# Two more seven-product pairs in the down projection, six raw weight buffers and rings of five split weights

## The chip, the cores and the metric

The kernel runs on one core of one Trainium2 chip. The metric is device time in microseconds (us) of one execution. Times below come from three timed runs and from one profiled execution of the kernel before.

## The reference

The reference is one decoder layer in float32 on 256 tokens and 16 meta tokens. What matters here is its last part, the SwiGLU feed-forward network on 256 tokens with width 2048 and 5632 hidden channels:

```python
u = rmsnorm(h, attn_norm_w[l])
proj = u @ w_in[l]
...
h = h + jnp.concatenate([o_a, o_d], axis=-1) @ w_out[l]
u = rmsnorm(h, ffn_norm_w[l])
h = h + (jax.nn.silu(u @ w_gate[l]) * (u @ w_up[l])) @ w_down[l]
```

All weights are float32 and each is read once from memory.

## The kernel before

**A product in three matmuls.** Every float32 operand is split into `hi` (rounded to the matmul's type) and `lo` (the rest). A product of two blocks is then three matmuls: hi by hi, hi by lo, lo by hi. The activations are split once. A weight tile of 128 x 1024 numbers (512 KB) goes through three steps: a DMA that SP issues brings it into a buffer `raw` (`load_to`, L261), ACT casts it to `hi` (L274), and DVE subtracts to get `lo` (L275). There are `WR` = 4 buffers `raw` in one ring. The pairs of `hi` and `lo` stand in rings of `WS` = 4, and from the SwiGLU on `WS2` = 2 more, so six. `next_w` hands the next split weight to the matmuls; on each call it splits ahead as far as the ring goes and issues loads ahead (`load_to(pos[3] + WR - 1)`).

**Seven products for eight.** In the SwiGLU (chunks of 512 hidden channels, `chunk`) and in the down projection (two passes p = 0 and p = 1 over two column tiles of 512 each), the weights come in pairs: two channel blocks by two column tiles. `block` (L1367) multiplies such a pair with the two token blocks. An ordinary pair takes two split weights (called w, w in what follows), each used in 4 products, so 8 products or 24 matmuls. The pairs named in `SEVEN` (SwiGLU) and `DSEVEN` (down: 7, 9, 11, 13, 15, 17, 19 of the 22 pairs in each pass) take 7 products or 21 matmuls by a Strassen-like scheme. For that DVE forms sums of the two raw tiles (L291 to L294: `t` twice, then `s` twice, 128 x 512 each), and four split weights are made, in this order: the first raw tile (g), half of the second (u), `t`, `s`. It also needs sums of the activations. They are made by `side_forms` (L1318 to L1330: seven DVE instructions and two ACT casts) ahead of the pass, and used by both passes.

**What sets the order.** A generator-based task list (`tasks`) places side work between products while the program is written. Instructions on ACT and SP stay in that order; those on PE and DVE are put in their final order by a scheduler. Each engine then runs its own list in order, so an instruction that waits holds up all behind it on its engine. SP's list of DMAs is in order too.

**The matmuls** of chunks and of down stand on L1381, those of the first chunk on L1199. The first chunk is computed as two plain streams (gate, up), and its end, `ffn_task` (L1306 multiplies, `to_hT` transposes on L1277), runs while PE has begun the second chunk. Between the two passes of down, `down_mid` and `down_end` (L1504, L1516) finish the first two column tiles, SP writes them out (L1518), and `fetch_x1` loads the residual for the next two (L1484).

Of the kernel before, what the change touches and what calls it, by code (L numbers as in the profile page):

```python
# [8 lines left out]
F32 = mybir.dt.float32  # L9
# [6 lines left out]
P = 128  # L16
# [5 lines left out]
FFN = 5632  # L22
# [3 lines left out]
NCH = FFN // 512  # L26
# [3 lines left out]
KC = (0, 72, 144, T)  # L30
R1, R2 = 12, 10
WR, WS = 4, 4
WS2 = 2
WHOLE = 8
SEVEN = (2, 4, 6)
DSEVEN = (7, 9, 11, 13, 15, 17, 19)
# [130 lines left out]
def layer(tc, xT, aw, x, w_in, w_ba, w_out, w_gate, w_up, w_down, cmask, dist, par, out):  # L167
# [3 lines left out]
    def pool(name, bufs=1, space=None):  # L171
        cm = tc.tile_pool(name=name, bufs=bufs, **({"space": space} if space else {}))
        return cm, cm.__enter__()
# [8 lines left out]
    cm_w, wp = pool("wp")  # L182
# [7 lines left out]
    tasks = Tasks(PER_STEP)  # L190
# [13 lines left out]
    def act(out_, in_, func, **kw):  # L204

        act_table("silu_and_others" if func == AF.Silu else "natural_log_exp_and_others")
        S.activation(out_, in_, func, **kw)

    def mark(k, n=1):
        done[k] = done.get(k, 0) + n  # L210

    def at_least(k, n):
        return lambda: done.get(k, 0) >= n
# [20 lines left out]
    def w_tile(wv, q, c):  # L234
        return wv[:, 2 * q:2 * q + 2, 512 * c:512 * (c + 1)], 2, 512
# [4 lines left out]
    forms = [("w", i) for i in range(len(order))]  # L240
    for c in range(1, NCH):
        for q in range(KT // 2):
            i = len(order)
            order += [w_tile(wv, q, c) for wv in (wg_v, wu_v)]
            forms += [("w", i), ("w", i + 1)] if q not in SEVEN else [("g", i), ("u", i), ("t", i), ("s", i)]
    for c in (0, 2):
        for q in range(FFN // P // 2):
            i = len(order)
            order += [w_tile(wd_v, q, c + j) for j in range(2)]
            forms += [("w", i), ("w", i + 1)] if q not in DSEVEN else [("g", i), ("u", i), ("t", i), ("s", i)]  # L250
    raws, ready, sums_ = {}, {}, {}

    pos = [0, 0, 0, 0]
    more = []

    def load_to(n, parts=1, eng=nc.sync):
        while pos[0] < min(n, len(order)):
            src, a, b = order[pos[0]]
            raw = wp.tile([P, a, b], F32, tag="raw", bufs=WR, name=f"raw{pos[0]}")
            for i in range(0, a, a // parts):  # L260
                eng.dma_start(out=raw[:, i:i + a // parts], in_=src[:, i:i + a // parts])  # L261
            raws[pos[0]] = raw
            pos[0] += 1

    def split(raw, n, a, b, parts=1, rows=slice(0, None)):

        k = n % (WS + WS2) if more else 0
        if k < WS:
            hi, lo = (wp.tile([P, a, b], F32R, tag=t, bufs=WS, name=f"{t}{n}") for t in ("hi", "lo"))
        else:  # L270
            hi, lo = (more[0].tile([P, a, b], F32R, tag=f"{t}2", bufs=WS2, name=f"{t}{n}") for t in ("hi", "lo"))
        for j in range(0, a, a // parts):
# [31 lines left out]
    def next_w():  # L304
        i = pos[2]
        pos[2] += 1
        split_to(i + WS + (WS2 if more else 0))
        load_to(pos[3] + WR - 1)
        return ready.pop(i)


# [3 lines left out]
    nc.sync.dma_start(out=xr[0][:, 0:1, :], in_=xT[:, 0:1, :])  # L315
    nc.sync.dma_start(out=aw_sb, in_=aw)
    load_to(1, 2, S)

    act_table("natural_log_exp_and_others")
# [61 lines left out]
    for k in range(KT):  # L381
        src, w = xr[k // 8][:, k % 8, :], aw_sb[:, k:k + 1]
# [870 lines left out]
    hT = {}  # L1253
# [45 lines left out]
    def ffn_task(c, b, pg, pu):  # L1299
        g_ = yield from fpool[1].get(512)  # L1300
        act(g_, pg, AF.Silu, scale=rr[:, b:b + 1])
        mm.free()
        yield at_least(f"up{c}", 1)
        yield 1
        ps = pu[b]
        V.scalar_tensor_tensor(g_, ps, rr[:, b:b + 1], g_, ALU.mult, ALU.mult)  # L1306
        mm.free()
        yield 2
        yield from to_hT(c, b, g_)


# [2 lines left out]
    def side_forms(key, h, l, sh, sl):  # L1314

        v = yield from fpool[1].get(2, SEQ)
        w = yield from fpool[1].get(4, P)
        V.tensor_tensor(v, h, l, ALU.add)  # L1318
        a11, a21, a12, a22 = v[:, 0, 0:P], v[:, 0, P:SEQ], v[:, 1, 0:P], v[:, 1, P:SEQ]
        V.tensor_tensor(w[:, 0], a21, a22, ALU.add)  # L1320
        V.tensor_tensor(w[:, 1], w[:, 0], a11, ALU.subtract)
        V.tensor_tensor(w[:, 2], a11, a21, ALU.subtract)
        V.tensor_tensor(w[:, 3], a12, w[:, 1], ALU.subtract)
        yield 2
        h1, l1 = h[:, 0, P:SEQ], l[:, 0, P:SEQ]
        S.copy(h1, w[:, 0])
        S.copy(sh, w[:, 1:4])
        yield 1
        V.tensor_tensor(l1, w[:, 0], h1, ALU.subtract)
        V.tensor_tensor(sl, w[:, 1:4], sh, ALU.subtract)  # L1330
        fpool[1].free(2)
        sides[key] = [(h1, l1)] + [(sh[:, i], sl[:, i]) for i in range(3)]
        mark(f"side{key}")

    def side_tiles(i):
        return [fpool[0].tile([P, 3, P], F32R, tag=f"{n}{i}", name=f"{n}{i}") for n in ("sh", "sl")]
# [27 lines left out]
        yield 10  # L1364
        yield from to_hT(c, b, h_)

    def block(c, name, nq, seven, lhs, need, mid, end):  # L1367

        ring, other = rings[c % 2], rings[(c + 1) % 2]
        tasks.until(lambda: ring.live == 0)  # L1370
        x = [ring.now() for _ in range(4)]
        y = []
        n = nq - len(seven)
        left = {("x", i): 3 * (2 * n + (len(seven) if i < 3 else 0)) for i in range(4)}
        left.update({("y", i): 3 * len(seven) for i in range(4)})
        todo = dict(left)

        def product(bank, a, w):
            for l, r in ((a[0], w[0]), (a[0], w[1]), (a[1], w[0])):
                first, todo[bank] = todo[bank] == left[bank], todo[bank] - 1  # L1380
                PE.matmul((x if bank[0] == "x" else y)[bank[1]], l, r, start=first, stop=todo[bank] == 0)  # L1381

        for q in range(nq):
            k = 2 * q
            if need:
                tasks.until(need(k))
            if q not in seven:
                for col in range(2):
                    hi, lo = next_w()
                    for i in range(2):  # L1390
                        for b in range(2):
                            product(("x", 2 * col + b), lhs(k + i, b), (hi[:, i], lo[:, i]))
                            tasks.step()
                    if q == nq - 1:
                        end(col, x)
                continue
            if not y:
                tasks.until(lambda: other.live == 0)
                y += [other.now() for _ in range(4)]
            tasks.until(at_least(f"side{(name, q)}", 1))  # L1400
            s1, s2_, s3, s4 = sides[name, q]
            plan = (((("y", 0), lhs(k, 0), 0), (("x", 0), lhs(k + 1, 0), 1)), ((("x", 2), s4, 1),),
                    ((("y", 3), s1, 0), (("y", 2), s3, 1)), ((("y", 1), s2_, 0), (("x", 1), lhs(k + 1, 1), 1)))
            for part in plan:
                hi, lo = next_w()
                for bank, a, i in part:
                    product(bank, a, (hi[:, i], lo[:, i]))
                    tasks.step()
            if q == seven[-1]:
                mid(y)  # L1410
# [32 lines left out]
    for b in range(2):  # L1443
        tasks.spawn(ffn_task(0, b, pg[b], pu), urgent=True)
    pu += stream(range(KT - 4), lhs_u, last=False)
    for i, q in enumerate(SEVEN):
        k = slice(2 * q, 2 * q + 2)
# [61 lines left out]
    def down_end(p, b, c, ps):  # L1509
# [8 lines left out]
            nc.sync.dma_start(out=out[P * b:P * (b + 1), o:o + w], in_=r_)  # L1518
        rings[(NCH + p) % 2].free()

    def down_side(i, q):
        if i < len(SEVEN):
            sh, sl = side_tiles(i)
        else:
            if i == len(SEVEN):

                yield at_least(f"hT{NCH - 1}", 3)
                t = fpool[0].tile([P, 6 * P], F32R, tag=f"hT{NCH - 1}", name=f"side{q}")
            else:
                o = 8 * SEQ + 6 * P * (i - len(SEVEN) - 1)  # L1530
                t = rest[:, o:o + 6 * P]
            sh, sl = (t[:, 3 * P * j:3 * P * (j + 1)].rearrange("p (a b) -> p a b", b=P) for j in range(2))
        k = slice(2 * q % 4, 2 * q % 4 + 2)
        c = q // 2
        yield at_least(f"hT{c}", 2 if c < WHOLE else 3)
        h, l = (hT[c][:, 0], hT[c][:, 1]) if c < WHOLE else hT[c]
        yield from side_forms(("h", q), h[:, k, :], l[:, k, :], sh, sl)
# [3 lines left out]
    for i, q in enumerate(DSEVEN):  # L1541
        tasks.spawn(down_side(i, q), delay=24)
    tasks.spawn(fetch_x1(0), delay=24)
    for p in range(2):
        def end(col, x):
            for b in range(2):
                tasks.spawn(down_end(p, b, col, x[2 * col + b]), urgent=True)

        def mid(y):
            tasks.until(lambda: fpool[1].live <= 1)  # L1550
            t = [fpool[1].now((512,)) for _ in range(3)]
            S.copy(t[0], y[0])
            tasks.spawn(down_mid(p, y, *t), delay=0, urgent=True)

        block(NCH + p, "h", FFN // P // 2, DSEVEN, lhs_h, need_h, mid, end)
        if p == 0:
            tasks.spawn(fetch_x1(1), delay=12)
    tasks.until(lambda: not tasks.list)
# [66 lines left out]
```

## Time and profile before

| | value |
|---|---|
| median of three runs | 1223.23 us (1222.27 to 1226.79) |
| profiled execution | 1224.38 us, its span 1222.6 us |
| mean granted TensorE clock | 1.000 |
| PE busy | 1209.2 us (99%), 7316 matmuls |
| DVE busy | 983.6 us (80%) |
| ACT busy | 692.3 us (57%) |
| DMA | 228.54 MB, mean 187 GB/s |

The span is the time from the first to the last instruction. Busy time of PE is modelled from the starts of pipelined matmuls. In time order the span holds the mixer with its projections (to about 510 us), the first chunk (to 558 us), ten more chunks (to 983 us), pass p = 0 of down (to 1099 us) and pass p = 1 (to 1218 us). "Released by" in a wait means the instruction or DMA whose end let the waiting one start.

### The profile page before, as it was taken

The numbers are of one execution on the slowest core, as the hardware profiler recorded it, in microseconds if no ns is written. First come the engines' busy times: TensorE is split into PE (matmuls) and PEld (weight loads), VectorE is DVE, ScalarE is ACT, GpSimd is POOL, SyncE is SP. The second block draws the span as 40 slices with busy tenths as digits, with TensorE's granted clock in tenths as the row PEclk, the third lists the DMA queues.
The fourth block names the chain that finished last, engine by engine and source line by source line (L and its number), as shares of the span: only waits on it lengthen the run. The fifth ranks groups of instructions, "written<-read, shape, count | busy, mean of one in ns | idle before, by whom it ended". The sixth has DMA issues, their size and how long they took to land.

```text
span 1222.6 us, 19223 instructions
## 1 busy us (share of the span) xinstructions
PE 1209.2 (99%) x7316; PEld 1060.0 (87%) x7316; DVE 983.6 (80%) x1573; ACT 692.3 (57%) x1087; POOL 6.1 (0%) x14
## 2 busy tenths in 40 slices
PE   9999999999999999999999999999999999999998
PEld 7999999999999988887888888888888888888876
DVE  7989974686676666668889988998998899886686
ACT  7674465275776665455555556555555665553552
POOL 0000000000000000000000000000000000000000
PEclk9999999999999999999999999999999999999999
DMA  8466564344544645685665665566566565567543
GB/s 293 124 207 195 145 187 121 112 124 145 172 140 139 229 162 178 191 277 167 196 206 186 195 218 190 192 204 217 166 208 216 187 211 197 201 225 276 181 164 133
DMA packets 151869, 228.54 MB, mean 187 GB/s; under 512 B 11736, under 2 KB 72672, under 8 KB 151264
## 3 DMA queue, kind: packets, MB, share of 16 engines
q1 hardware_dynamic: 151232, 226.78, 57.4%
q8 instruction: 57, 0.93, 0.3%
q10 hardware_dynamic: 544, 0.52, 0.1%
q14 instruction: 36, 0.29, 0.1%
HBM read 221.83 MB, written 5.45 MB: 186 GB/s over the span
## 4 chain that ended last, share of the span: by engine, by line
PE 85%; DVE 7%; DMA 4%; ACT 2%; issue 1%; SPq 0%; DVEq 0%; ACTq 0%
PE aux L1381 25%; PE mm L1152 23%; PE mm L1381 21%; PE mm L1199 10%; DVE lo L275 3%; DMA raw<-in_w_down_dram 3%; ACT hi L274 1%; PE aux L1100 1%; PE aux L1055 1%; DMA raw<-in_w_in_dram 0%; PE mm L1277 0%; DVE s L293 0%; DMA raw<-in_w_up_dram 0%; DVE r L581 0%; PE aux L1277 0%
## 5 line engine op out<-in xcount | busy, mean ns | idle before, releaser
L274 ACT CAST hi<-raw 128x1024 fp32r<-128x1024 f32 (+1 forms) x412 | 405.1, 996 | 325.0 <-PE mm L1152 93.3
L275 DVE TENSOR_TENSOR lo<-raw,hi 128x1024 fp32r<-128x1024 f32 (+1 forms) x412 | 470.6, 1153 | 141.6 <-ACT hi L274 139.1
L1152 PE MATMUL mm<-xh,hi 128*128 128x272 f32 (+2 forms) x896 | 258.4, 289 | 0.0
L1152 PE MATMUL mm<-xl,hi 128*128 128x272 f32 (+2 forms) x896 | 255.9, 286 | 0.9 <-DVE xl L384 0.6
L1152 PE MATMUL mm<-xh,lo 128*128 128x272 f32 (+2 forms) x896 | 255.0, 286 | 1.0 <-DVE lo L275 1.0
L1152 PEld LDWEIGHTS mm<-xl,hi 128*128 128x128 f32 x896 | 168.5, 188 | 2.2 <-DVE xl L384 2.0
L1152 PEld LDWEIGHTS mm<-xh,hi 128*128 128x128 f32 x896 | 168.6, 188 | 2.1 <-issue 1.5
L1152 PEld LDWEIGHTS mm<-xh,lo 128*128 128x128 f32 x896 | 168.2, 188 | 1.6 <-DVE lo L275 1.4
L1381 PE MATMUL aux<-hi,uh 128*128 128x512 f32 x260 | 101.6, 391 | 0.0
L1381 PE MATMUL mm<-hi,uh 128*128 128x512 f32 x260 | 101.6, 391 | 0.0
L1381 PE MATMUL aux<-hi,ul 128*128 128x512 f32 x260 | 101.3, 390 | 0.0
L1381 PE MATMUL mm<-hi,ul 128*128 128x512 f32 x260 | 101.2, 389 | 0.0
L1381 PE MATMUL aux<-lo,uh 128*128 128x512 f32 x260 | 101.2, 389 | 0.0
L1381 PE MATMUL mm<-lo,uh 128*128 128x512 f32 x260 | 101.2, 389 | 0.0
L1381 PE MATMUL aux<-hi,hT 128*128 128x512 f32 x216 | 70.2, 389 | 0.0
L1381 PE MATMUL mm<-hi,hT 128*128 128x512 f32 x216 | 70.0, 389 | 0.0
L274 ACT CAST hi<-s 128x1024 fp32r<-128x1024 f32 x44 | 46.3, 1053 | 38.0 <-DVE s L294 34.5
L291 DVE TENSOR_TENSOR t<-raw,raw 128x512 f32<-128x512 f32 x44 | 30.2, 687 | 38.7 <-DMA raw<-in_w_down_dram 25.2
L274 ACT CAST hi<-t 128x1024 fp32r<-128x1024 f32 x44 | 46.3, 1053 | 26.2 <-DVE t L292 11.3
L1381 PEld LDWEIGHTS aux<-hi,ul 128*128 128x128 f32 x260 | 48.8, 188 | 10.2
L1381 PEld LDWEIGHTS mm<-hi,ul 128*128 128x128 f32 x260 | 48.8, 188 | 10.2
L1381 PEld LDWEIGHTS mm<-hi,uh 128*128 128x128 f32 x260 | 48.8, 188 | 10.0
(418 smaller groups left out, 2046.8 us busy)
## 6 DMA issues: line engine op xcount, KB each, us to landing
raw<-in_w_in_dram SPq DMA_DIRECT2D x111, 512.0 KB, 3.6
raw<-in_w_gate_dram SPq DMA_DIRECT2D x88, 512.0 KB, 3.7
raw<-in_w_up_dram SPq DMA_DIRECT2D x88, 512.0 KB, 4.4
raw<-in_w_down_dram SPq DMA_DIRECT2D x88, 512.0 KB, 4.6
raw<-in_w_out_dram SPq DMA_DIRECT2D x32, 512.0 KB, 4.2
x<-x1d SPq DMA_DIRECT2D x8, 256.0 KB, 4.8
xr<-in_xT_dram SPq DMA_DIRECT2D x7, 272.0 KB, 5.8
out_dram<-x SPq DMA_DIRECT2D x6, 256.0 KB, 5.1
```

Source lines behind the costliest of these rows:

```text
L274: S.copy(hi[:, js], raw[:, js])
L275: V.tensor_tensor(lo[:, js], raw[:, js], hi[:, js], ALU.subtract)
L291: V.tensor_tensor(t[:, 0], u[:, 0], g[:, 0], ALU.subtract)
L1055: PE.matmul(pss[m][:, cut[n]], q[ms, P * n:P * (n + 1)], k[ms, 0:NK[n]], start=True, stop=True)
L1100: PE.matmul(po[:, n, :], l, r, start=(j == 0), stop=(j == 1 + n))
L1152: PE.matmul(acc[c][:, 0:n], a[:, k, cs], b[:, kt, t0:T], start=(kt == 0 and i == 0), stop=(kt == KT - 1 and i == 2))
L1199: PE.matmul(acc[b], l, r[:, i % 2, :], start=(first and i == 0 and j == 0), stop=(last and i == len(kts) - 1 and j == 2))
L1381: PE.matmul((x if bank[0] == "x" else y)[bank[1]], l, r, start=first, stop=todo[bank] == 0)
```

## The change

Five things change. (1) In pass p = 1 of down, pairs 3 and 5 become seven-product pairs as well (`EXTRA`), so that pass has nine. (2) Their activation sums are formed in p = 1 itself (`extra_side`), after pairs 0 and 1 of that pass, and written over the hidden channels of those pairs, which nothing reads any more. (3) Two raw buffers are added from the SwiGLU on (`WR2` = 2), and loads are issued two further ahead. (4) The rings of split weights go from six to five there (`WS2` = 1). (5) In `ffn_task` the transposes of the first chunk's result are placed six steps later (`yield 8` for `yield 2`).

```diff
--- before.py
+++ after.py
@@ -30,7 +30,8 @@
 KC = (0, 72, 144, T)
 R1, R2 = 12, 10
 WR, WS = 4, 4
-WS2 = 2
+WS2, WR2 = 1, 2
+EXTRA = (3, 5)
 WHOLE = 8
 SEVEN = (2, 4, 6)
 DSEVEN = (7, 9, 11, 13, 15, 17, 19)
@@ -247,7 +248,8 @@
         for q in range(FFN // P // 2):
             i = len(order)
             order += [w_tile(wd_v, q, c + j) for j in range(2)]
-            forms += [("w", i), ("w", i + 1)] if q not in DSEVEN else [("g", i), ("u", i), ("t", i), ("s", i)]
+            seven = q in DSEVEN or c == 2 and q in EXTRA
+            forms += [("g", i), ("u", i), ("t", i), ("s", i)] if seven else [("w", i), ("w", i + 1)]
     raws, ready, sums_ = {}, {}, {}
 
     pos = [0, 0, 0, 0]
@@ -256,7 +258,10 @@
     def load_to(n, parts=1, eng=nc.sync):
         while pos[0] < min(n, len(order)):
             src, a, b = order[pos[0]]
-            raw = wp.tile([P, a, b], F32, tag="raw", bufs=WR, name=f"raw{pos[0]}")
+            if more and pos[0] % (WR + WR2) >= WR:
+                raw = more[0].tile([P, a, b], F32, tag="raw2", bufs=WR2, name=f"raw{pos[0]}")
+            else:
+                raw = wp.tile([P, a, b], F32, tag="raw", bufs=WR, name=f"raw{pos[0]}")
             for i in range(0, a, a // parts):
                 eng.dma_start(out=raw[:, i:i + a // parts], in_=src[:, i:i + a // parts])
             raws[pos[0]] = raw
@@ -305,7 +310,7 @@
         i = pos[2]
         pos[2] += 1
         split_to(i + WS + (WS2 if more else 0))
-        load_to(pos[3] + WR - 1)
+        load_to(pos[3] + WR + (WR2 if more else 0) - 1)
         return ready.pop(i)
 
 
@@ -1305,7 +1310,7 @@
         ps = pu[b]
         V.scalar_tensor_tensor(g_, ps, rr[:, b:b + 1], g_, ALU.mult, ALU.mult)
         mm.free()
-        yield 2
+        yield 8
         yield from to_hT(c, b, g_)
 
 
@@ -1364,7 +1369,7 @@
         yield 10
         yield from to_hT(c, b, h_)
 
-    def block(c, name, nq, seven, lhs, need, mid, end):
+    def block(c, name, nq, seven, lhs, need, mid, end, past=None):
 
         ring, other = rings[c % 2], rings[(c + 1) % 2]
         tasks.until(lambda: ring.live == 0)
@@ -1393,6 +1398,8 @@
                             tasks.step()
                     if q == nq - 1:
                         end(col, x)
+                if past:
+                    past(q)
                 continue
             if not y:
                 tasks.until(lambda: other.live == 0)
@@ -1518,6 +1525,15 @@
             nc.sync.dma_start(out=out[P * b:P * (b + 1), o:o + w], in_=r_)
         rings[(NCH + p) % 2].free()
 
+    def extra_side(q):
+
+        i = EXTRA.index(q)
+        sh, sl = (hT[i // 2][:, j, 2 * i % 4:2 * i % 4 + 2, :].rearrange("p a b -> p (a b)")[:, 0:3 * P]
+                  .rearrange("p (a b) -> p a b", b=P) for j in range(2))
+        k = slice(2 * q % 4, 2 * q % 4 + 2)
+        h = hT[q // 2]
+        yield from side_forms(("h", q), h[:, 0, k, :], h[:, 1, k, :], sh, sl)
+
     def down_side(i, q):
         if i < len(SEVEN):
             sh, sl = side_tiles(i)
@@ -1552,7 +1568,11 @@
             S.copy(t[0], y[0])
             tasks.spawn(down_mid(p, y, *t), delay=0, urgent=True)
 
-        block(NCH + p, "h", FFN // P // 2, DSEVEN, lhs_h, need_h, mid, end)
+        def past(q):
+            if p == 1 and q < len(EXTRA):
+                tasks.spawn(extra_side(EXTRA[q]))
+
+        block(NCH + p, "h", FFN // P // 2, DSEVEN if p == 0 else EXTRA + DSEVEN, lhs_h, need_h, mid, end, past)
         if p == 0:
             tasks.spawn(fetch_x1(1), delay=12)
     tasks.until(lambda: not tasks.list)
```

Three places show how the instructions now stand. The first is DVE in pass p = 1, from the sums of one seven-product pair on. Before (pair 11: raw_11700 and raw_11738 are its tiles g and u, raw_11698 is the second tile of pair 10, raw_11756 the first of pair 12):

```order
L291 TENSOR_TENSOR t_11768<-raw_11738,raw_11700 128x512
L292 TENSOR_TENSOR t_11768<-raw_11738 128x512
L293 TENSOR_TENSOR s_11769<-raw_11738,t_11768 128x512
L275 TENSOR_TENSOR lo_11753<-raw_11698,hi_11752 128x1024
L294 TENSOR_TENSOR s_11769<-raw_11700,s_11769 128x512
L275 TENSOR_TENSOR lo_11765<-raw_11700,hi_11764 128x1024
L275 TENSOR_TENSOR lo_11778<-raw_11738,hi_11777 128x512
L275 TENSOR_TENSOR lo_11792<-t_11768,hi_11791 128x1024
L275 TENSOR_TENSOR lo_11802<-s_11769,hi_11801 128x1024
L275 TENSOR_TENSOR lo_11818<-raw_11756,hi_11817 128x1024
```

After (pair 11: raw_11727 and raw_11752 are its tiles g and u, raw_11671 and raw_11715 those of pair 10, s_11737 is the sum of pair 9):

```order
L296 TENSOR_TENSOR t_11819<-raw_11752,raw_11727 128x512
L297 TENSOR_TENSOR t_11819<-raw_11752 128x512
L280 TENSOR_TENSOR lo_11779<-s_11737,hi_11778 128x1024
L298 TENSOR_TENSOR s_11820<-raw_11752,t_11819 128x512
L299 TENSOR_TENSOR s_11820<-raw_11727,s_11820 128x512
L280 TENSOR_TENSOR lo_11795<-raw_11671,hi_11794 128x1024
L280 TENSOR_TENSOR lo_11807<-raw_11715,hi_11806 128x1024
L280 TENSOR_TENSOR lo_11816<-raw_11727,hi_11815 128x1024
L280 TENSOR_TENSOR lo_11832<-raw_11752,hi_11831 128x512
L280 TENSOR_TENSOR lo_11846<-t_11819,hi_11845 128x1024
```

The sums of a pair now stand ahead of the last split (`lo<-s`) of the pair before and ahead of both splits of the ordinary pair between, where before they stood after the first of these.

The second place is SP's queue where pass p = 0 is written out (out_dram<-x_00, x_01), the residual for p = 1 is fetched (x_10, x_11) and the weights of p = 1 come in. Before:

```order
L261 DMA raw_11379<-in_w_down_dram 128x2x512
L1518 DMA out_dram<-x_00_10669 128x512 x2
L261 DMA raw_11405<-in_w_down_dram 128x2x512
L1518 DMA out_dram<-x_01_10677 128x512 x2
L261 DMA raw_11427<-in_w_down_dram 128x2x512
L261 DMA raw_11445<-in_w_down_dram 128x2x512
L1484 DMA x_10_11459<-x1d 128x512 x2
L1484 DMA x_11_11462<-x1d 128x512 x2
L261 DMA raw_11469<-in_w_down_dram 128x2x512
```

After (raw_11425 and raw_11482 are tiles g and u of pair 5, raw_11484 the first of pair 6):

```order
L266 DMA raw_11359<-in_w_down_dram 128x2x512
L266 DMA raw_11377<-in_w_down_dram 128x2x512
L1525 DMA out_dram<-x_00_10663 128x512 x2
L266 DMA raw_11403<-in_w_down_dram 128x2x512
L1525 DMA out_dram<-x_01_10671 128x512 x2
L266 DMA raw_11425<-in_w_down_dram 128x2x512
L1491 DMA x_10_11470<-x1d 128x512 x2
L1491 DMA x_11_11473<-x1d 128x512 x2
L266 DMA raw_11482<-in_w_down_dram 128x2x512
L266 DMA raw_11484<-in_w_down_dram 128x2x512
```

One load moved from between the writes and the fetch to ahead of the writes.

The third place is PE at the start of the second chunk, with the transposes (mm<-ident,gact) of the first chunk's result. Before:

```order
L1381 MATMUL aux_6787<-hi_6674,ul 128x512
L1277 MATMUL mm_6813<-ident,gact_6609 128x128 x4
L1381 MATMUL aux_6788<-hi_6674,uh 128x512
L1381 MATMUL aux_6788<-lo_6675,uh 128x512
L1277 MATMUL mm_6818<-ident,gact_6612 128x128 x4
L1381 MATMUL aux_6788<-hi_6674,ul 128x512
```

After:

```order
L1386 MATMUL aux_6779<-hi_6714,uh 128x512
L1386 MATMUL aux_6779<-lo_6715,uh 128x512
L1386 MATMUL aux_6779<-hi_6714,ul 128x512
L1386 MATMUL aux_6780<-hi_6714,uh 128x512
L1386 MATMUL aux_6780<-lo_6715,uh 128x512
L1386 MATMUL aux_6780<-hi_6714,ul 128x512
L1282 MATMUL mm_6841<-ident,gact_6607 128x128 x4
L1282 MATMUL mm_6846<-ident,gact_6610 128x128 x4
```

The two groups of transposes went from behind the 21st and the 23rd matmul of the chunk to behind the 30th.

## The prediction

> **What bounds the kernel now.** I read the page's first lines, then the waits of PE, the chain in order of time, and the instructions of DVE and SP in the stretches that these point to.
>
> ```profile
> span 1222.6 us, 19223 instructions
> PE 1209.2 (99%) x7316; PEld 1060.0 (87%) x7316; DVE 983.6 (80%) x1573; ACT 692.3 (57%) x1087; POOL 6.1 (0%) x14
> ```
>
> The profiled execution took 1224.38 us, so 1.8 us lie outside the span; it stands 1.15 us above the median of the runs. PE works 99% of the span. A gain therefore has to be fewer matmuls or fewer of PE's few waits; 0.5% of the time, 6.1 us, is about what a measurement of this kernel tells from no change. The waits of PE from 540 us on are two:
>
> ```profile
> PE mm L1381 <- DVE lo L275: 3.3, 3, 1.8
> PE mm L1277 <- DVE gact L1306: 1.3, 1, 1.3
> PEld mm L1381 <- DVE lo L275: 4.5, 3, 2.2
> ```
>
> The first row and the third are the same three stops, seen by the matmul and by its weight load. All lie in pass p = 1; they cost between 3.3 and 4.5 us, I take 3.9. In the chain, the stretch before them is not PE's:
>
> ```profile
> 1142.74 7.23 DMA raw<-in_w_down_dram
> 1153.72 1.75 DVE lo L275 x2
> 1155.49 5.61 DMA raw<-in_w_down_dram
> 1166.62 6.34 DMA raw<-in_w_down_dram
> 1176.72 1.75 DVE lo L275 x2
> 1178.48 5.95 DMA raw<-in_w_down_dram
> 1188.19 1.75 DVE lo L275 x2
> 1189.95 6.77 DMA raw<-in_w_down_dram
> 1199.93 2.81 PE mm L1381 x11
> 1206.82 10.89 PE mm L1381 x48
> ```
>
> It is a loop of DVE and DMA: a split frees a buffer, the load into it lands, the next sums read it. One turn on DVE:
>
> ```profile
> 1173.09 0.69 DVE L291 TENSOR_TENSOR t<-raw,raw 128x512 f32<-128x512 f32 x1 [3.08 <-DMA raw<-in_w_down_dram]
> ...
> 1184.55 0.69 DVE L291 TENSOR_TENSOR t<-raw,raw 128x512 f32<-128x512 f32 x1 [2.69 <-DMA raw<-in_w_down_dram]
> 1185.16 0.68 DVE L292 TENSOR_TENSOR t<-raw 128x512 f32<-128x512 f32 x1
> 1185.76 0.69 DVE L293 TENSOR_TENSOR s<-raw,t 128x512 f32<-128x512 f32 x1
> 1186.37 1.22 DVE L275 TENSOR_TENSOR lo<-raw,hi 128x1024 fp32r<-128x1024 f32 x1
> 1187.50 0.68 DVE L294 TENSOR_TENSOR s<-raw,s 128x512 f32<-128x512 f32 x1
> 1188.11 1.82 DVE L275 TENSOR_TENSOR lo<-raw,hi 128x1024 fp32r<-128x1024 f32 x2
> 1189.84 1.22 DVE L275 TENSOR_TENSOR lo<-t,hi 128x1024 fp32r<-128x1024 f32 x1
> 1190.98 1.22 DVE L275 TENSOR_TENSOR lo<-s,hi 128x1024 fp32r<-128x1024 f32 x1
> 1192.11 1.22 DVE L275 TENSOR_TENSOR lo<-raw,hi 128x1024 fp32r<-128x1024 f32 x1
> 1196.84 0.69 DVE L291 TENSOR_TENSOR t<-raw,raw 128x512 f32<-128x512 f32 x1 [3.51 <-DMA raw<-in_w_down_dram]
> ```
>
> A turn takes 11.5 us (1173.09 to 1184.55) and 12.3 us (to 1196.84). PE needs 45 matmuls for the same two pairs (24 and 21). The last row of the chain gives 10.89/48 = 0.227 us a matmul, so 10.2 us. DVE falls behind by more than a microsecond a turn until PE stops. DVE itself works 9 us of the turn; the rest is the wait for tile u.
>
> **The change part by part.**
>
> *Products.* Two pairs lose three matmuls each: 6 x 0.227 = 1.36 us saved, on PE's path. They add, on DVE, 4 sums and 2 splits each (4 x 0.60 + 2 x 1.14 = 4.7 us by the starts above) and seven instructions for the activation sums; on ACT four casts. All that lies beside the products of pairs 0 to 5, where DVE has room now, since those pairs are ordinary; I cost it at nothing there. If that cover goes, the two extra turns of the loop are what it costs (below).
>
> *Transposes of the first chunk.* PE stood until L1306 had come:
>
> ```profile
> 563.29 0.74 DVE L1306 SCALAR_TENSOR_TENSOR gact<-mm,rr,gact 128x512 f32<-128x512 f32 x1
> 564.08 0.66 PE L1277 MATMUL mm<-ident,gact 128*128 128x128 f32 x4 [1.34 <-DVE gact L1306]
> ```
>
> Now they stand nine matmuls (2.0 us) later, and DVE does L1306 five instructions earlier. The 1.3 us go whole; with the slow restart perhaps 1.7. I take 1.5 saved (1.3 to 1.7). Next late would be the split of pair 2, which stopped nothing here: the waits above name no other line.
>
> *Loop of pass p = 1.* In the new order the sums stand directly behind `lo<-t` of the pair before. With six buffers, tile u of the next pair takes the buffer of the second tile of the ordinary pair (six loads back), and that is freed by the seventh DVE instruction of the turn. From the sums' start: 0.61 + 0.60 + 1.14 + 0.60 + 0.60 + 1.14 + 1.22 = 5.9 us. In the old order it was tile u itself, freed after 5.4 us (1184.55 to 1189.93). So six buffers do not take the load out of the turn: they only let it start from another place. What counts is how long that load takes. It is the second of two issued 1.1 us apart. Loads that stood so:
>
> ```profile
> raw<-in_w_up_dram SPq DMA_DIRECT2D x1, 512.0 KB, 5.3
> ...
> raw<-in_w_down_dram SPq DMA_DIRECT2D x1, 512.0 KB, 6.2
> ...
> raw<-in_w_down_dram SPq DMA_DIRECT2D x1, 512.0 KB, 3.5
> ```
>
> The first two rows are the first and the last (at 681.4 and 1141.0 us) of eight such loads with a known landing, from issue to landing; the eight lie between 4.2 and 6.2 us, mean 5.2. The third is a load alone (at 1026.4 us). With 5.2 us and 0.15 us for issue and start, a turn takes 11.3 us, 1.1 more than PE's 10.2. So the wait stays, a little shorter than now.
>
> How long PE then stands hangs on the lead at the start. With `p = 1` begun at 0, pairs 0 to 2 end at 3 x 5.44 = 16.3 us, pair 3 at 21.1, pair 5 at 31.3. Pair 4's second tile is cast when PE has freed its slot (tile g of pair 3 done, 17.7) and split by 20.3; tile u of pair 7 lands at 25.6; sums and splits put the first weight of pair 6 at 30.4, 0.9 us ahead of its use. Each further turn takes 1.06 us off that: 0.2 us late at pair 8, then 1.06 us at each of pairs 10 to 18. Together 5.5 us of stops in place of 3.9: 1.6 us lost. The two extra pairs thus gain 0.68 us each and add a turn each that loses more. Bounds: with loads of 4.2 us the turn is 10.3 us and all stops go (3.9 gained); with 6.2 us, 2.06 us a turn, 12.5 us of stops (8.6 lost). I take the mean, since the eight are spread evenly.
>
> The residual's fetch stands ahead of tile u of pair 5 in SP's queue; before, a load behind it was issued 12.7 us into the pass:
>
> ```profile
> 1107.42 4.26 SPq L1484 DMA_DIRECT2D x<-x1d  x4
> 1111.74 90.87 SPq L261 DMA_DIRECT2D raw<-in_w_down_dram  x33
> ```
>
> Needed by 16.4 us at the latest, that leaves 3.7 us. I cost it at nothing, since one load fewer stands before it; late by 2 us, it adds 2 us.
>
> *Loop of pass p = 0.* The same order holds from pair 13 on, three turns. The lead at pair 14 is 1.6 us by the same working; 3 x 1.06 leaves a stop of about 0.5 us at pair 18. Bounds 0 and 3.6.
>
> *Rings of five.* In the chunks no stop on a split is there now. One weight late in the fourth chunk:
>
> ```profile
> 716.27 1.05 ACT L274 CAST hi<-raw 128x1024 fp32r<-128x1024 f32 x1 [0.63 <-PE mm L1381]
> 717.36 1.22 DVE L275 TENSOR_TENSOR lo<-raw,hi 128x1024 fp32r<-128x1024 f32 x1
> 722.99 6.12 PE mm L1381 x27
> ```
>
> Its slot came free at 716.2, the split was done at 718.6, and PE used it after three matmuls of the third row, at 723.7: 5 us ahead. With five slots it is freed one ordinary weight (12 x 0.227 = 2.7 us) later, so 2.3 us remain. A chunk has three seven-product pairs with ordinary ones between and after, so only the sums of the third (pair 6) follow the loop's rule; the first weight of pair 5 behind them keeps about 0.9 us. DVE's waits for tile u in the chunks are now 9, up to 2.1 us:
>
> ```profile
> DVE t L291 <- DMA raw<-in_w_up_dram: 10.9, 9, 2.1
> ```
>
> I take 0.5 us over ten chunks, with 0 and 3 as bounds.
>
> *The sum.* -1.4 - 1.5 + 1.6 + 0.5 + 0.5 = -0.3 us against the profiled 1224.4, so 1224.1; against the median, 1222.9 us.
>
> On loads, the Trainium skill (DMA: Bandwidth & Descriptors, "Anatomy of one DMA") puts a transfer at about 2.0 us plus its bytes at 436 GB/s, 3.2 us for 512 KB by estimate, and its "Rules for kernel authors" say that a load issued early and awaited late hides that cost. By them a turn would be 9.3 us, no stop would be left, and the sum would be that of the first rival. The load alone at 3.5 us agrees with the figure; the second of two at 5.2 us does not, and it is the one that the turn holds.
>
> **The rivals.**
>
> *The loop's waits vanish.* Loads issued further ahead could run ahead of DVE, if the second of two lands in 4.2 us. For it: one of the eight did, and loads in the chunks wait little. Against it: the order now asks for the sums earlier. No stops in p = 1 and none elsewhere: -1.4 - 1.5 - 3.9 = -6.8, 1217.6 profiled, 1216.4 us at the median, just past the 0.5%.
>
> *The loop slows.* Four loads now go out within 3 us (buffers freed at 4.7, 5.9, 7.0 and 7.6 us of the turn); the row at 6.2 us above stood in just such a group. With 5.9 us a turn is 12.0 us, stops in p = 1 near 10.5 us, in p = 0 some 3: the sum is +6.7, 1230 us at the median. It decides against the kernel from about 5.3 us a load on.
>
> *Rings of five stop PE in the chunks.* If each chunk's pair 5 comes 1.5 us later than worked out, that is 0.6 us and more in ten chunks; with 0.9 us, 9 us in all: 1231 us. For it: the lead falls from 5 to 2.3 us. Against it: PE has no such stop now.
>
> **How the numbers follow.** Forecast 0.54 (its own range 1219 to 1227), waits vanish 0.22, loop slows 0.16, rings 0.08. The range 1216.5 to 1229 leaves out the far half of the last two and the far half of the first. Faster by over 0.5%: half of the first rival, 0.11. Slower: a third of the second (over 1229.3) and three quarters of the third, 0.11. Within: 0.78.
>
> **What would show it.** PE: 7310 instructions (six fewer). The wait for L1306 gone. In p = 1, sums (L296) waiting for down's tiles eight times, 2 to 3 us each, a turn of 11.3 us, and PE's stops on `lo` some 5.5 us in five or six places, the first near pair 8 or 10. In the chunks nearly none. I am wrong if the sums no longer wait and the turn is 10.2 us (then the first rival), or if stops stand at pair 5 of the chunks.

## The result and the profile after

The changed kernel took 1235.62 us (median of four runs, 1233.28 to 1238.24) and the kernel before 1223.47 us beside it. The ratio is 1.0093 with a 95% interval of 1.0078 to 1.0109: slower by 11.4 us by this ratio (12.15 us between the medians), where -0.3 us was forecast. The profiled execution took 1236.86 us. The page's first lines after:

```profile
span 1235.1 us, 19251 instructions
PE 1212.2 (98%) x7310; PEld 1057.8 (86%) x7310; DVE 996.9 (81%) x1599; ACT 696.7 (56%) x1095; POOL 6.1 (0%) x14
```

The six matmuls are gone (7310 in place of 7316), and the span is still 12.5 us longer. The waits of PE and of its weight load from 540 us on:

```profile
PE mm L1386 <- DVE lo L280: 8.0, 10, 0.9
PE aux L1386 <- DVE lo L280: 5.5, 8, 0.9
```

```profile
PEld mm L1386 <- DVE lo L280: 12.5, 11, 1.4
PEld aux L1386 <- DVE lo L280: 9.4, 9, 1.4
```

The wait for `gact` (L1306 before) is gone, as the transposes' move meant it to be. In its place stand some twenty stops for a `lo`, where there were three. Each is short, 1.4 us at most by the weight load; their number makes the sum.

Which stage has them is worked out from the matmuls' starts. The time from the first matmul of a stage to the first of the next, less 0.2267 us (the steady distance of two matmul starts) for each matmul of its products, is what was lost there. Some 0.9 us of transposes stand in each stage but the last, so 0.9 is the floor, and 0.2 in p = 1. Each figure comes from one profile.

| lost in us | second chunk | chunks 3 to 11, each | p = 0 | p = 1 |
|---|---|---|---|---|
| before | 2.48 | 0.9 | 0.91 | 4.36 |
| changed kernel | 0.92 | 0.9 | 4.74 | 15.61 |

So -1.56 in the second chunk, +3.83 in p = 0, +11.25 in p = 1 and -1.36 for six matmuls: 12.2 us. The other 0.3 us of the 12.5 lie ahead of the chunks.

The chain in order of time, in p = 1 (columns: start, duration, what):

```profile
1112.04 6.86 DMA raw<-in_w_down_dram
1122.69 2.36 DVE lo L280 x2
1125.07 5.77 DMA raw<-in_w_down_dram
1134.77 2.37 DVE lo L280 x2
1137.15 6.21 DMA raw<-in_w_down_dram
1147.27 2.36 DVE lo L280 x2
1149.65 5.96 DMA raw<-in_w_down_dram
1159.54 2.36 DVE lo L280 x2
1161.92 5.42 DMA raw<-in_w_down_dram
...
1198.24 6.27 DMA raw<-in_w_down_dram
1209.71 5.51 PE mm L1386 x23
```

It is the loop that the prediction described, now from the pass's first seven-product pair to its last. Two splits of the ordinary pair end, a load starts into the buffer that they freed, and the next sums read what it brings. From 1125.07 to 1198.24 are six turns, 12.2 us each, where PE needs 10.2. One turn on DVE:

```profile
1143.48 0.69 DVE L296 TENSOR_TENSOR t<-raw,raw 128x512 f32<-128x512 f32 x1 [3.48 <-DMA raw<-in_w_down_dram]
1144.08 0.69 DVE L297 TENSOR_TENSOR t<-raw 128x512 f32<-128x512 f32 x1
1144.69 1.22 DVE L280 TENSOR_TENSOR lo<-s,hi 128x1024 fp32r<-128x1024 f32 x1
1145.94 0.69 DVE L298 TENSOR_TENSOR s<-raw,t 128x512 f32<-128x512 f32 x1
1146.66 0.69 DVE L299 TENSOR_TENSOR s<-raw,s 128x512 f32<-128x512 f32 x1
1147.27 4.09 DVE L280 TENSOR_TENSOR lo<-raw,hi 128x1024 fp32r<-128x1024 f32 x4
1151.28 1.22 DVE L280 TENSOR_TENSOR lo<-t,hi 128x1024 fp32r<-128x1024 f32 x1
1155.74 0.69 DVE L296 TENSOR_TENSOR t<-raw,raw 128x512 f32<-128x512 f32 x1 [3.24 <-DMA raw<-in_w_down_dram]
```

The four splits of the row at 1147.27 are both of the ordinary pair, then g and u. PE needs the first of them next, and it stands behind a sum that waits 3.2 to 3.5 us for a tile of the pair after. The buffer is free 6.2 us into the turn (the load's issue at 1149.65), and the load takes another 6.0.

### The profile page after: what moved, and what is told of

It is laid out like the page before. It is cut to its first block, busy times and chain, and to the rows that moved or that the text cites. A ratio compares the mean times of both kernels' runs of the same rounds, so it can differ in the third digit from the quotient of the medians.

```text
span 1235.1 us, 19251 instructions
## 1 busy us (share of the span) xinstructions
PE 1212.2 (98%) x7310; PEld 1057.8 (86%) x7310; DVE 996.9 (81%) x1599; ACT 696.7 (56%) x1095; POOL 6.1 (0%) x14
## 4 chain that ended last, share of the span: by engine, by line
PE 80%; DVE 9%; DMA 6%; ACT 2%; issue 2%; SPq 0%; DVEq 0%; ACTq 0%
PE mm L1157 23%; PE aux L1386 22%; PE mm L1386 19%; PE mm L1204 11%; DMA raw<-in_w_down_dram 5%; DVE lo L280 5%; ACT hi L279 1%; DVE t L296 1%; DVE s L298 1%; PE aux L1105 1%; DVE t L297 1%; PE aux L1060 1%; DMA raw<-in_w_in_dram 0%; PE mm L1282 0%; DVE r L586 0%
## 5 line engine op out<-in xcount | busy, mean ns | idle before, releaser
L280 DVE TENSOR_TENSOR lo<-raw,hi 128x1024 fp32r<-128x1024 f32 (+1 forms) x412 | 464.1, 1151 | 122.0 <-ACT hi L279 118.9
L1386 PE MATMUL aux<-hi,hT 128*128 128x512 f32 x232 | 75.8, 390 | 0.0
L280 DVE TENSOR_TENSOR lo<-s,hi 128x1024 fp32r<-128x1024 f32 x46 | 56.2, 1222 | 13.1 <-ACT hi L279 13.0
L1386 PE MATMUL mm<-hi,hT 128*128 128x512 f32 x196 | 64.5, 390 | 0.0
```

The source lines that it names most:

```text
L280: V.tensor_tensor(lo[:, js], raw[:, js], hi[:, js], ALU.subtract)
```

## The experiments

Each ratio is to the kernel before, run again beside it. "Lost" is the figure of the table above. Theory A was that the place of the sums, ahead of the ordinary pair's splits, puts a load into every turn. Its rivals: the two extra pairs are the cost (B in the first set), or the shorter ring (C).

**The transposes alone** (kernel before, `yield 8` for `yield 2` in `ffn_task`).

> The kernel before with one part of the change alone: the transposes six steps later. Both theories: the second chunk is 1.5 us shorter (43.96 to 42.4 us), all other stages as before, so 1221.7 us.

Ratio 0.9986 (0.9974 to 0.9999). The second chunk lost 0.92 us in place of 2.48. This part does what it should. Pass p = 1, which this edit does not touch, lost 5.14 us in place of 4.36, so a pass that holds this loop varies by some 0.8 us between two profiles.

**The pairs without the buffers.**

```diff
-WS2, WR2 = 1, 2
+WS2, WR2 = 2, 0
```

> The changed kernel with the buffers of before (four raw, rings of six), so the two extra pairs and the later transposes alone. Theory A (the cost is the place of the sums together with the load inside the turn, and comes from buffers and rings): the order of before comes back, pass p = 0 loses 0.9 us over its matmuls as before (4.7 in the changed kernel), pass p = 1 some 5 to 8 us (15.6 in the changed kernel), in all 1221 to 1226 us. Theory B (the two extra pairs are the cost): pass p = 1 stays near 15 us, in all 1230 us or more.

Ratio 1.0018 (0.9998 to 1.0038). p = 0 lost 0.89 us, as before; p = 1 lost 9.73, over the 5 to 8 expected by theory A and far from the 15 of theory B; the median of 1227.49 us lies between their forecasts too. Two turns more of the old loop, which is also longer than PE's, cost 5.4 us of stops for 1.36 us of matmuls.

**The buffers without the pairs.**

```diff
-EXTRA = (3, 5)
+EXTRA = ()
```

> The changed kernel without the two extra pairs: six raw buffers, rings of five, later transposes. Theory A: pass p = 0 keeps its 4.7 us of loss, and pass p = 1 loses about 2 us at each turn from pair 9 or 11 on, near 10 us; in all about 1232 us. Theory B: pass p = 1 loses no more than the 4.4 us of before; in all at most 1226 us.

Ratio 1.0052 (1.0034 to 1.0070). p = 0 lost 4.09 us and p = 1 9.85, near theory A's figures. So the loss in p = 0 belongs to the buffers, rings and their order. In p = 1 either part costs about 5.4 us (4.36 to 9.73, and to 9.85), and both together 11.25: within the 0.8 us of two profiles they add up. Theory B is half right there.

**The sums behind the splits.** An edge for the scheduler, in down alone, keeps the four sums on DVE behind the last split of the ordinary pair before them:

```diff
+                behind = last[0].ins.name
...
+                for one in four:
+                    if i >= DOWN:
+                        tc.add_manual_dep(one.ins, behind, ...)
```

> The changed kernel with one thing more: in down, the four sums of a pair may not stand ahead of the splits of the ordinary pair before it. Theory A: the load of tile u then has most of a turn (some 10 us) in place of 4 to 6 us, DVE no longer waits for it, the turn is PE's 10.2 us, and the stops of both passes go: about 1216.4 us. Theory C (the lead lost with the ring of five is the cost, whatever stands ahead): stops of a microsecond and more stay at each ordinary pair, and the time stays at 1230 us or more.

Ratio 0.9951 (0.9936 to 0.9966), median 1218.14 us. p = 1 lost 0.16 us and p = 0 1.45. Its DVE in the same stretch:

```profile
1142.18 0.68 DVE L298 TENSOR_TENSOR t<-raw,raw 128x512 f32<-128x512 f32 x1
...
1148.74 3.72 DVE L281 TENSOR_TENSOR lo<-raw,hi 128x1024 fp32r<-128x1024 f32 x3 [1.04 <-ACT hi L280]
1152.38 0.68 DVE L298 TENSOR_TENSOR t<-raw,raw 128x512 f32<-128x512 f32 x1
```

In this stretch the sums wait for nothing, the turn is 10.20 us, and DVE's only wait is for a cast, which follows PE. The work on each engine, the buffers and the rings are those of the changed kernel. The order of DVE's list is all that was changed between 1.0093 and 0.9951, and theory C falls.

**The fetch out of the way.**

```diff
-            tasks.spawn(fetch_x1(1), delay=12)
+            tasks.spawn(fetch_x1(1), delay=84)
```

> The changed kernel with the residual's fetch for p = 1 72 products later, so that it no longer stands in SP's queue ahead of tile u of pair 5. Theory A (the start of the loop decides, and each microsecond of it comes out at the end): tile u of pair 5 is issued near 6 us into the pass in place of 10.4 and its sums start near 1115.5 in place of 1119.0; the split that frees the buffer for pair 7 comes 3 us earlier, and pass p = 1 loses 12 to 13 us in place of 15.6; the time is 0.25% less than the changed kernel's, ratio to before 1.0065. Theory B (the turn alone decides, the later turns take the lead back): the loss stays at 15 to 16 us, ratio 1.009.

Ratio 1.0080 (1.0060 to 1.0099), which holds both forecasts. The profile decides: p = 1 lost 12.11 us in place of 15.61. SP's queue at the start of the pass, in the changed kernel and then here:

```profile
1105.84 0.40 SPq L266 DMA_DIRECT2D raw<-in_w_down_dram  x1
1107.68 4.27 SPq L1491 DMA_DIRECT2D x<-x1d  x4
1112.04 2.32 SPq L266 DMA_DIRECT2D raw<-in_w_down_dram  x3
```

```profile
1104.99 0.43 SPq L266 DMA_DIRECT2D raw<-in_w_down_dram  x1
1106.60 0.93 SPq L1525 DMA_DIRECT2D out_dram<-x  x2
1107.63 8.51 SPq L266 DMA_DIRECT2D raw<-in_w_down_dram  x4
```

Tile u of pair 5 leads the last row of the first, at 1112.04. In the second it is the second load of the row at 1107.63. The first splits of the chain then stand at

```profile
1121.48 2.36 DVE lo L280 x2
```

where the changed kernel has them at 1122.69. Its pass began at 1101.68 us and this one at 1103.46, so they start 18.0 us into the pass in place of 21.0. Where every later turn is too long, a late start is never made up: 3.0 us at the start were 3.5 us at the end, the rest from turns of 12.1 us in place of 12.2.

**The load without followers.**

```diff
+            if pos[0] in held:
+                nc.sync.dma_start(out=hold[:, :], in_=raw[0:1, 0, 0:16])
```

> The changed kernel with a 64-byte DMA in SP's queue behind each load of a tile u in down; it reads that tile, so SP holds the next two loads back until tile u has landed. Theory A (the two loads issued behind it make the load of tile u slow): it lands 4.2 to 4.6 us after its issue in place of 5.9 to 6.3, the turn of DVE in p = 1 is 10.5 to 11 us in place of 12.2, pass p = 1 loses 3 to 7 us in place of 15.6; ratio to before 0.998 to 1.003. Theory B (the load ahead of it makes it slow): it keeps its 6 us, the turn stays at 12 us or more, ratio 1.009 or above.

Ratio 1.0020 (1.0009 to 1.0031); p = 1 lost 6.61 us. The chain:

```profile
1122.08 4.96 DMA raw<-in_w_down_dram
1130.84 2.36 DVE lo L284 x2
1133.22 4.75 DMA raw<-in_w_down_dram
1141.89 2.36 DVE lo L284 x2
1144.27 5.01 DMA raw<-in_w_down_dram
...
1189.58 4.84 DMA raw<-in_w_down_dram
```

The seven loads of this chain from 1122 us on have a mean of 5.0 us; the seven of the changed kernel from 1125 us on 5.95. The turn is 11.25 us (1122.08 to 1189.58, six turns). So the two loads issued behind tile u are worth about 1 us of its time, and theory A's 4.2 to 4.6 us was too low: 1.5 us over the 3.5 of a load alone remain with one load ahead of it. Two loads of the kernel before that stood so, with nothing behind them for 3.5 us and more, took 5.0 and 4.8 us (issued at 1027.5 and 1036.4 us). Neither theory holds whole. Not all of the 9.0 us that the pass gained is the load's: six turns of 0.95 us are 5.7, and the scheduler also put the first two of these splits ahead of the last sum of their turn, so that they ended 21.5 us into the pass in place of 23.4.

**The order with the old buffers, without and with the extra pairs.** Both have the edge of the fourth experiment and the later transposes, four raw buffers and rings of six.

> The kernel before with the later transposes and the sums of down behind the ordinary splits; four raw buffers, rings of six, no extra pairs. Theory A (the place of the sums decides, the buffers matter little): tile u is freed about 4.3 us into a turn and its load takes 5 to 6, a turn of 9.7 to 10.7 us, nearly no stops in p = 1: its loss falls from 4.4 to about 1 us, ratio to before 0.996. Theory B (six buffers are needed for that): the loss stays at 3 us or more, ratio 0.998 or above.

> As the run before it, with the two extra pairs as well. Theory A: 1.4 us less than that run, ratio to before 0.995. Theory B: two turns more at 10.7 us or more, loss of 4 us or more in p = 1, ratio 0.998 or above.

Ratios 0.9962 (0.9949 to 0.9975) and 0.9956 (0.9941 to 0.9971). p = 1 lost 0.16 us in both, and the pass was 1.36 us shorter with the extra pairs (115.08 and 113.72 us). The pairs give just their six matmuls once nothing waits, and the two raw buffers give nothing that can be measured (0.9951 in the fourth experiment, 0.9956 here).

**Tile u by another queue.** POOL issues the loads of tile u in down.

```diff
-                eng.dma_start(...)
+                (G if pos[0] in second else eng).dma_start(...)
```

> The changed kernel with the loads of tile u of down's seven-product pairs issued by POOL, which is idle there, on a DMA queue of its own; they no longer stand in SP's order behind the residual's fetch either. Theory A (the load of tile u is slow because the load ahead of it in the same queue is served first): it lands 3.5 to 4.5 us after its issue, the turn in p = 1 is 10.5 to 11 us, pass p = 1 loses 2 to 6 us in place of 15.6, ratio to before 0.997 to 1.002. Theory B (the loads share the memory and the DMA engines whatever their queue): tile u keeps 5.5 us or more, the turn stays near 12 us, and only the start is earlier: a loss of 11 to 13 us, ratio 1.006 or above.

Ratio 1.0243 (1.0221 to 1.0265): on theory B's side, and far beyond its figures for the turn and the loss. p = 0 lost 11.7 us and p = 1 29.1. The load of tile u at 1143.3 us and the next one of SP, from issue to landing; then POOL's issues:

```profile
raw<-in_w_down_dram POOLq DMA_DIRECT2D x1, 512.0 KB, 8.3
```

```profile
raw<-in_w_down_dram SPq DMA_DIRECT2D x1, 512.0 KB, 8.1
```

```profile
1143.32 0.72 POOL L267 DMA_DIRECT2D raw<-in_w_down_dram  x1 [13.65 <-DVE lo L281]
1158.13 0.72 POOL L267 DMA_DIRECT2D raw<-in_w_down_dram  x1 [14.09 <-DVE lo L281]
1172.66 0.72 POOL L267 DMA_DIRECT2D raw<-in_w_down_dram  x1 [13.81 <-DVE lo L281]
```

Tile u landed in 8.3 us, the load behind it in 8.1; in the changed kernel they took 6.0 and 6.7 (issued at 1149.65 and 1150.79). The turn went to 14.7 us (1143.32 to 1172.66, two turns) and the loss with it, which is the loop once more, with a longer load. The granted clock of PE fell to 0.95 in this pass (1.00 in the changed kernel's); DVE and the load make up the turn, not PE.

**The order with the least memory**: the fourth experiment's kernel with `WS2, WR2 = 1, 0`.

> The changed kernel with the sums of down behind the ordinary splits, four raw buffers and rings of five: 8 KB per partition less than before or after. Theory A (the place of the sums is all that matters): as with six buffers, p = 1 loses 0.2 us, p = 0 about 1.5, ratio to before 0.995. Theory B (either the sixth slot or the two raw buffers have to give the slack): stops come back in p = 1, 3 us or more, ratio 0.998 or above.

Ratio 0.9991 (0.9974 to 1.0008). Down is as theory A had it (p = 1 lost 0.16 us, p = 0 1.42). But the last chunk lost 5.53 us in place of 0.92 (and the one before it 1.56), in a place that neither theory looked at. Waits of DVE in the chunks, in the changed kernel and then here:

```profile
DVE t L296 <- DMA raw<-in_w_up_dram: 9.0, 10, 1.6
```

```profile
DVE t L298 <- DMA raw<-in_w_up_dram: 18.9, 15, 4.4
```

In the chunks the sums may still be placed early, and with four raw buffers and rings of five one of them waited 4.4 us with three splits behind it. So either the sixth slot or the two buffers are needed as long as the chunks keep that order.

## Why the prediction was wrong

The step that failed is the price of the loop: +1.6 us for p = 1 and +0.5 us for p = 0 stood in the sum, and +11.25 and +3.83 us came. The other terms held.

- **Products**: right. The 1.36 us stand between the seventh and eighth experiments.
- **Transposes**: right, 1.56 us for 1.5.
- **Rings of five**: 0 in the chunks for 0.5 us, the lower of its bounds. In p = 0 they may cost 0.3 us: with the sums behind the splits that pass lost 1.45 us with five slots and six buffers, 1.14 with six slots and four. The seventh experiment, with the same six and four, lost 0.92, so 0.3 is little more than two profiles differ.
- **Loop of p = 1**: the mechanism was right (the six buffers do not take the load out of the turn, they only let it start from another place), and the size of its turn was off, 11.3 us for 12.2. Most of that is the load: 5.2 us was taken, the mean of eight loads that stood in several situations. In the new order tile u always has two loads close behind it, and that was the situation of the row of 6.2 us, which the prediction named in a rival and let into its sum only as one of the eight. Measured: 5.95 us. Five loads of the loop itself stood in the prediction's chain as well, at 7.23, 5.61, 6.34, 5.95 and 6.77 us: in other company, but all of them over 5.2 (one before them, at 1129.79 us, took 4.91). The rest of the difference is DVE's part ahead of the load, 6.2 us for 5.9. At each of some seven turns 0.9 us more is 6 us.
- **The start of p = 1**: the fetch ahead of tile u of pair 5 was costed at nothing, and it cost 3.0 us at the start. The tile was to be there 16.4 us into the pass. The pass's first matmul starts at 1101.68 us, and by the chain's first row the tile's wait ended at 1118.90 (1112.04 and 6.86): 17.2 us. It was issued at 10.4 us, earlier than the 12.7 of the load in the row before, but its load took 6.86 us where 3.7 were allowed. The 16.4 us also asked for too little. They are what pair 4's first weight needs; the forecast's lead rests on pair 4's second tile being split by 20.3 us. From the first sum to the end of that split are 6.0 us (1119.02 to 1125.05), because the sums of pair 5 stand ahead of it, so the lead needed tile u by about 14.3. In the changed kernel that split ended at 23.4 us; without the fetch, in the fifth experiment, at 20.4. The first stop was at pair 4, not at 8 or 10.
- **Loop of p = 0**: 0.5 us forecast, 3.8 measured, by the same turn: its last three sums started at 1051.56, 1063.47 and 1075.63 us, 11.9 and 12.2 apart.

The sum with these sizes: p = 1 lost 5.5 us in the forecast; 6 for the turn and 3.0 for the fetch make 14.5, and 15.4 were measured over the floor. The rival that the loop slows named the cause and priced it at 1230 us. It kept the forecast's lead at the start, and therefore came 5 us short in p = 1; at 0.16 it also had too little of the chance. The rival that the waits vanish counted on loads of 4.2 us, and the loop's loads took 5.4 to 6.3. The fourth experiment took the waits away by the order instead and came out near that rival's -6.8 us: 0.9951 of 1223.2 us is -6.0, with an interval of -7.8 to -4.2.

On loads, the Trainium skill (DMA: Bandwidth & Descriptors, "Anatomy of one DMA") gives by estimate 3.2 us for 512 KB, from a fit to DMAs that GpSimd issues; the loads here are issued by SP. The first load of each group comes near it (3.5 us for the one issued at 1148.5 us); tile u at 5.95 us does not.

The best version run has the sums behind the splits and both extra pairs. With six buffers (0.9951) or four (0.9956) it beats both kernels. The two cannot be told apart, and by its time neither can the one without the pairs (0.9962); the pairs show in the length of the pass alone.

## What to carry to other kernels

Where an engine's list is in order, look at what stands behind each instruction that can wait for a transfer: an instruction for later work that is placed early turns its own wait into one of everything behind it. Another buffer takes a load out of a loop only if it is freed before the loop's waiting instruction, so work out the turn, from the freeing instruction to the one that waits, before counting buffers. If the turn is longer than the bound engine's period, everything that delays the first turn comes out whole at the end, and the price of the load must come from rows in the same company, not from a mean.

## What the hardware showed

A load of 512 KB took 3.5 us alone. The first of a group of four in p = 1 took 3.5 to 3.9 us although the others followed. The second, issued 1.1 us behind the first, took 5.95 us with two more issued behind it within 1.7 us, and 5.0 us in the sixth experiment, where those two were held back; a later load thus made an earlier one of the same queue slower. Issued by POOL on a second queue, in the same company, it took 8.3 us, and the one behind it 8.1 in place of 6.7: the second queue sped up neither. Why both were slower was not tried.
